# A later issue of packed query/key copies, and memory attention in three parts, in a hybrid transformer layer on one Trainium2 core

## The chip, the cores and the metric

The kernel runs on one core of one Trainium2 chip. The metric is the device time of one execution in microseconds (us), lower is better. Five engines work beside each other: PE (TensorE, matmuls; its weight loads are listed as PEld), DVE (VectorE), ACT (ScalarE), POOL (GpSimd) and SP (SyncE, which here only issues DMAs). Each takes its instructions in the order in which the program lists them for it.

## What is computed

One layer over 4096 tokens of width 1024: `x + W_out(concat(branches))`, where all branches read one normalised input.

```python
h = rms(x); g_u,g_v,g_gate, a_q,a_k,a_v,a_gate, m_q,m_gate = split(h @ w_in)
y_g = chunked_gmlp(g_u, rms(g_v)) * silu(g_gate)              # 4 heads x 64
y_a = dilated_attention(rms(a_q), rms(a_k), a_v) * silu(a_gate)   # 8 heads x 64, dilations 1, 4, 16
y_m = memory_attention(rms(m_q), mem) * silu(m_gate)          # 4 heads x 64, 256 memory tokens
x = x + concat([y_g, y_a, y_m]) @ w_out
```

The dilated attention is a softmax over a causal window for each of three dilations, mixed by the softmax denominators. The memory attention is a softmax over the 256 memory tokens.

## The kernel before, in words

The tokens are worked through in 32 tiles of 128. Every fp32 product is made of fp16 high and low parts, so that a projection (`proj`, L219) of one tile and 512 columns is 24 matmuls, accumulated in one PSUM buffer of the tag "pj", of which there are two.

Four stages follow each other. **Pass A** (L384) normalises and transposes each tile, writes it to DRAM, and projects the attention values (`pv`) and the queries and keys of heads 0 to 3 (`pq`). **Pass B** (`pass_b`, L678) loads the transposed tiles again and projects the queries and keys of heads 4 to 7 (`pqb`) and the attention gate (`pag`). **Pass C** (`pass_c`, L847) has three projections a tile: `pc1` (L855: the gMLP's v and the memory queries, wC1), `pc2` (L881, wC2) and `pc3` (L891, wC3). The last two belong to the tile that is LAG = 2 behind. The **output stage** (L934) adds the branches and projects with W_out. Beside passes B and C a side stream (`attn_all`, L660) computes the dilated attention: a maximum for each query (`attn_max`, L465: matmuls `pa`, DVE's L483) and the main part (`attn_main`, L533: matmuls `s`, DVE's mask L578, ACT's exponential L580 and cast `ph` L529, POOL's rest `pl` L530, matmuls `o`). `merge` (L59) advances the side stream by so many steps each time the pass yields, and gives its instructions a priority 400 places ahead.

The order on every engine is made by a scheduler ahead of the run: it simulates the program and gives an engine, of the instructions that are ready in that simulation, the one that comes first in program order (shifted by the priority). On the chip an engine then keeps that list, whether its next instruction is ready or not.

**Queries and keys** (`qk_out`, L292, in passes A and B). ACT copies the projection out of PSUM (L257) and squares it (L259); DVE sums (L261); POOL raises to the power -1/2 (L269); DVE multiplies (L276, L278); ACT casts the high half (`cast` below, L296), DVE makes the low half (L297). SP then issues a DMA that transposes `hl` into half of the staging tile `stg` (L299). ACT copies this half, its tokens regrouped by residue, into `stp` (L300). In every odd tile SP issues three stores of the pair of tiles to DRAM: L304 (keys), L305 (queries), both from `stg`, and L306 (packed, from `stp`). `stg` has two buffers, `stp` one. After every eighth tile of pass A `load_max` loads head 0's part of this back.

**Attention to the memory** (`mem_attn`, L776, in pass C, run after pc1). First part: ACT makes the high half `qd` (L779), DVE the low half in `q2t` (L780; a single buffer), SP issues the DMA transpose of `qd` (L784); matmuls `mpa` (L789) and DVE's L791 find each query's maximum, L792 writes it into `q2t`, and SP issues the DMA transpose of `q2t` (L793). Then a yield. Second part: the score matmuls `ms` (L802 and L804, the latter reads the transposed `q2t`), the exponential (L814), cast (L815), rest (L816), matmuls `mo` (L822 to L826), and the division (L829, L830). Then pc2 and pc3 of the tile two behind. The PSUM copy of pc1, `rw_c` (L257), has two buffers, and the memory queries are read out of it until L780.

Of the kernel before, what the change touches and what calls it, by code (L numbers as in the profile page):

```python
# [2 lines left out]

# [15 lines left out]
P = 128  # L19
T = 4096  # L20
D = 1024
NT = T // P
KT = D // P
# [17 lines left out]
R16 = 16  # L41
# [30 lines left out]
def tile_hybrid_layer(ctx, tc, x, mem, norm_gain, w_in, gv_gain, wsT, gb, aqg, akg,  # L72
# [146 lines left out]
    def proj(ps, xt, w, n, c=0):  # L219
        for k in range(KT):  # L220
            for a, b in ((0, 0), (0, 1), (1, 0)):
                TE.matmul(ps[:, :n], xt[:, a, k, :], w[:, b, k, c:c + n],  # L222
                          start=(k == 0 and a == 0 and b == 0), stop=(k == KT - 1 and a == 1))


    def load_rows(pool, src, nm):
# [62 lines left out]
    sk = ctx.enter_context(tc.tile_pool(name="sk", bufs=2))  # L289
    pm = ctx.enter_context(tc.tile_pool(name="pm", bufs=2))  # L290

    def qk_out(pool, ps, n, g, scs, stgs):  # L292
        stg, stp = stgs
        qn = qk_split(pool, ps, 8, scs, f"q{g}_{n}", agn, 4)
        hl = pool.tile([P, 8, 2, HD], F16, name=f"hl{g}_{n}", tag="hl", bufs=2)
        S.copy(hl[:, :, 0, :], qn)  # L296
        V.tensor_sub(hl[:, :, 1, :], qn, hl[:, :, 0, :])  # L297
        half = slice((n % 2) * P, (n % 2 + 1) * P)
        Q.dma_start_transpose(stg[:, :, half], hl.rearrange("p s a c -> p (s a c)"))  # L299
        S.copy(stp[:, :, half].rearrange("p s (r j) -> p s r j", r=R16),  # L300
               stg[:, :, half].rearrange("p s (j r) -> p s r j", r=R16))
        if n % 2 == 1:
            cc = slice((n - 1) * P, (n + 1) * P)
            Q.dma_start(kn_d[g][:, :, cc].rearrange("s p t -> p s t"), stg[:, 4:8, :])  # L304
            Q.dma_start(qn_d[g][:, :, cc].rearrange("s p t -> p s t"), stg[0:64, 0:4, :])  # L305
            Q.dma_start(qkp_d[g][:, :, cc].rearrange("s p t -> p s t"), stp)  # L306

    def stages(n):
        return (pm.tile([P, 8, 256], F16, name=f"stg{n}", tag="stg", bufs=2),
# [27 lines left out]
    with tc.tile_pool(name="pA", bufs=2) as pA:  # L337
# [44 lines left out]
        stg = None  # L382
        mTs = sk.tile([P, 2, 2, KT, P], F16, name="mTs", tag="q1", bufs=1)
        for n in range(NT):  # L384
# [46 lines left out]
                stg = stages(f"A{n}")  # L431
            qk_out(pm, ps, n, 0, scQ0, stg)
            if n % 8 == 7:
                load_max(0, (n - 7) * P, (n + 1) * P)
            tick()
            if n == 5:
# [237 lines left out]
    LAG = 2  # L674
# [3 lines left out]
    def pass_b():  # L678
        xTs = {}
        wQ1, scQ1 = got("wQ1")  # L680
        stg = None
        for n in range(NT + LAG):
            if n < NT:
                xT = sk.tile([P, 2, KT, P], F16, name=f"xTb{n}", tag="xT", bufs=4)
                Q.dma_start(xT.rearrange("p a k t -> p (a k t)"), xT_d[n])
                xTs[n] = xT
                ps = ps_tile("pj", [P, 512], F32, f"pqb{n}")
                proj(ps, xT, wQ1, 512)
                if n % 2 == 0:
                    stg = stages(f"B{n}")  # L690
                qk_out(pm, ps, n, 1, scQ1, stg)
                yield
            tick()
            if n == 2:
                wAG, scAG = got("wAG")
                for i in range(2):
                    V.tensor_scalar_mul(hsc[:, i:i + 1], scAG[i][:, 2:3], 0.5)
                    V.tensor_mul(fag[:, i:i + 1], hsc[:, i:i + 1], scV[i][:, 0:1])
                    V.tensor_scalar_mul(fag[:, i:i + 1], fag[:, i:i + 1], 2.0 ** -4)
            if n >= LAG:  # L700
                m = n - LAG
                ps = ps_tile("pj", [P, 512], F32, f"pag{m}")
                proj(ps, xTs.pop(m), wAG, 512)
                sg = pm.tile([P, 512], F32, name=f"sg{m}", tag="sg", bufs=2)
                for i in range(2):
                    S.activation(sg[:, i * 256:(i + 1) * 256], ps[:, i * 256:(i + 1) * 256],
                                 AF.Tanh, scale=hsc[:, i:i + 1])
                V.scalar_tensor_tensor(sg, sg, 1.0, ps, ALU.add, ALU.mult)
                Q.dma_start(ag_d[m], sg)
                yield  # L710
            if n == 6:
                start_job("wC1", "w1", (C_GV, C_MQ), ng, nga)
            if n == 16:
                start_job("wC3", "wc", (C_MG,), ng, nga)
            if n == NT - 1 + CS:
                start_job("wC2", "w2", (C_GU, C_GG), ng, nga, gap=1)
# [59 lines left out]
    def mem_attn(n, qn):  # L776
# [5 lines left out]
            qms[0] = pm.tile([P, 2, 2, 4, P], F16, name=f"qm{n}", tag="stg", bufs=2)  # L782
        Q1m, Q2m = qms[0][:, n % 2, 0], qms[0][:, n % 2, 1]
        Q.dma_start_transpose(Q1m, qd.rearrange("p s a c -> p (s a c)"))  # L784
        m4 = pm.tile([P, 4], F32, name=f"m4{n}", tag="m4")
        for hp in range(2):
            pa = ps_tile("pa", [P, 2, 256], F32, f"mpa{n}_{hp}")
            for i in range(2):
                TE.matmul(pa[:, i, :], Q1m[:, 2 * hp + i, :], K1m[:, 2 * hp + i, :],  # L789
                          start=True, stop=True)  # L790
            V.tensor_reduce(m4[:, 2 * hp:2 * hp + 2], pa, AX.X, ALU.max)  # L791
        V.tensor_scalar(q2t[:, :, 64], m4, -(2.0 ** -15), msg[:, 3:4], ALU.mult, ALU.add)  # L792
        Q.dma_start_transpose(Q2m, q2t.rearrange("p s c -> p (s c)"))  # L793
        yield
        o = ps_tile("po", [P, 4, 65], F32, f"mo{n}")
        for hp in range(2):
            st = ps_tile("ps", [P, 2, 2, P], F32, f"ms{n}_{hp}")
            for i in range(2):
                h = 2 * hp + i
                for b in range(2):  # L800
                    kk = slice(b * P, (b + 1) * P)
                    TE.matmul(st[:, i, b, :], K1m[:, h, kk], Q1m[:, h, :], start=True,  # L802
                              stop=False)
                    TE.matmul(st[:, i, b, :], K2m[:, h, kk], Q2m[0:65, h, :], start=False,  # L804
                              stop=True)
            if not pools:
                e = at.tile([P, 512], F32, name=f"me{n}_{hp}", tag="e", bufs=4)
                ph = at.tile([P, 512], F16, name=f"mph{n}_{hp}", tag="ph", bufs=4)
                pl = at.tile([P, 512], F16, name=f"mpl{n}_{hp}", tag="pl", bufs=4)
            else:  # L810
                e = pools[0].tile([P, 512], F32, name=f"me{n}_{hp}", tag="fx", bufs=3)
                phl = pools[0].tile([P, 2, 512], F16, name=f"mp{n}_{hp}", tag="fx", bufs=3)
                ph, pl = phl[:, 0, :], phl[:, 1, :]
            S.activation(e, st.rearrange("p a b q -> p (a b q)"), AF.Exp, scale=msg[:, 2:3])  # L814
            S.copy(ph, e)  # L815
            G.tensor_sub(pl, e, ph)  # L816
            for i in range(2):
                h = 2 * hp + i
                for b in range(2):
                    c = (2 * i + b) * P  # L820
                    v = Vm[:, b, h, :]
                    TE.matmul(o[:, h, 0:65], ph[:, c:c + P], v[:, 0:65], start=(b == 0),  # L822
                              stop=False)
                    TE.matmul(o[:, h, 0:64], ph[:, c:c + P], v[:, 66:130], start=False,
                              stop=False)
                    TE.matmul(o[:, h, 0:65], pl[:, c:c + P], v[:, 0:65], start=False,  # L826
                              stop=(b == 1))
        rd = pm.tile([P, 4], F32, name=f"rd{n}", tag="rd")
        V.reciprocal(rd, o[:, :, 64])  # L829
        V.tensor_tensor(ym[n], o[:, :, 0:64], bcast(rd, HD), ALU.mult)  # L830
        yield

    ym, vns = {}, {}
    o1 = []
# [12 lines left out]
    def pass_c():  # L847
        xTs = {}
        for n in range(NT + LAG):
# [15 lines left out]
            if n == 1:  # L865
                wC2, scC2 = got("wC2")
                V.tensor_scalar_mul(fz[:, 0:1], scC2[1][:, 2:3], 0.5)
                V.tensor_mul(fz[:, 1:2], fz[:, 0:1], scC2[0][:, 2:3])
                V.tensor_scalar_mul(fz[:, 2:3], scC3[0][:, 2:3], 0.5)
                V.tensor_mul(fz[:, 3:4], fz[:, 2:3], scM[1][:, 0:1])  # L870
                V.tensor_scalar_mul(fz[:, 3:4], fz[:, 3:4], 2.0 ** -4)
            if n < NT:
                yield from mem_attn(n, qn)
            if n >= LAG:
                m = n - LAG
                xT = xTs.pop(m)
# [1 line left out]
                    zp = pm.tile([P, 2, 256], F32, name=f"z{m}", tag="sg", bufs=2)  # L878
                z = zp[:, m % 2]
                ps = ps_tile("pj", [P, 512], F32, f"pc2_{m}")  # L880
                proj(ps, xT, wC2, 512)  # L881
                S.activation(z, ps[:, 256:512], AF.Tanh, scale=fz[:, 0:1])
                V.scalar_tensor_tensor(z, z, 1.0, ps[:, 256:512], ALU.add, ALU.mult)
                V.scalar_tensor_tensor(z, z, fz[:, 1:2], ps[:, 0:256], ALU.mult, ALU.mult)
                yield
                ps = ps_tile("pj", [P, 512], F32, f"pc3_{m}")
                pg = ps[:, 256:512].rearrange("p (h c) -> p h c", c=HD)
                vn = vns.pop(m)
                for h in range(4):
                    TE.matmul(pg[:, h, :], wst_g[:, h, :], vn[:, h, :], start=True, stop=True)  # L890
                proj(ps, xT, wC3, 256)  # L891
                for h in range(4):
                    V.scalar_tensor_tensor(z[:, h * HD:(h + 1) * HD], pg[:, h, :],
                                           gbt[:, h:h + 1], z[:, h * HD:(h + 1) * HD],
# [3 lines left out]
                S.activation(zm, ps[:, 0:256], AF.Tanh, scale=fz[:, 2:3])  # L898
                V.scalar_tensor_tensor(zm, zm, 1.0, ps[:, 0:256], ALU.add, ALU.mult)  # L899
                zms[m] = zm  # L900
                yield
            if n >= LAG + MLAG:
                mem_gate(n - LAG - MLAG)
# [87 lines left out]
```

## Time and profile before

| | us |
|---|---|
| runs before, median of 3 | 2227.14 |
| lowest and highest of them | 2226.68 and 2234.79 |
| the profiled execution, its own time | 2231.72 |
| span of the profiled execution, first to last instruction | 2230.0 |
| PE busy in it | 2031.2 (91%) |
| DVE busy | 1459.8 (65%) |
| ACT busy | 1200.2 (54%) |
| POOL busy | 684.2 (31%) |
| mean granted TensorE clock | 0.966 of full speed |

A busy figure is the union of an engine's instructions. An idle time is given to the instruction that ended it, with what released that instruction behind an arrow. The profile tells the granted clock of TensorE as a share of 2.4 GHz; 0.5 is its lower level of 1.2 GHz. Stages, read from the first and last projections of each: pass A from 52 to 458 us, pass B to 1016, pass C to about 1870, then the output stage.

### The profile page before, as it was taken

Reading aid. Unit: us, or ns where it says so; the run is one execution under the profiler, and the core shown is the slowest. Engines: PE = TensorE matmul, PEld = TensorE weight load, DVE = VectorE, ACT = ScalarE, POOL = GpSimd, SP = SyncE. Lnnn points to the kernel's source line nnn. Section 1 sums busy time; section 2 is a strip of 40 time slices with the busy share of each in tenths; the row PEclk is TensorE's granted clock in tenths of the full one; section 3 lists DMA queues with packets and bytes.
Section 4 is the critical chain, followed back from the end, with each engine's and each line's share of the span. In section 5 each row is a group of like instructions: output and inputs, shape, how many; then the busy total and the mean of one; then the engine's idle time right before and its main releaser. Section 6 shows DMA issues by size and latency. Waiting matters only on the chain. (4 is left out here: it accounts for less than half of the span.)

```text
span 2230.0 us, 45732 instructions
## 1 busy us (share of the span) xinstructions
PE 2031.2 (91%) x17025; PEld 1297.4 (58%) x17025; DVE 1459.8 (65%) x4331; ACT 1200.2 (54%) x2048; POOL 684.2 (31%) x632
## 2 busy tenths in 40 slices
PE   5989989889889898899999898998997999999999
PEld 4435444334346455465676675775764766666676
DVE  7555564365657676477786677875876667777662
ACT  6666565343457577476565565664655763222221
POOL 1212212121035355253454453553543551000000
PEclk8999999999899999999999999999998999999999
DMA  7767676484565865755646447536435337777662
GB/s 228 198 152 207 167 187 163 115 212 121 153 145 136 205 147 130 202 119 146 167 98 138 116 94 169 114 94 151 97 90 124 89 97 219 222 218 220 205 187 75
DMA packets 468959, 341.00 MB, mean 153 GB/s; under 512 B 294400, under 2 KB 404096, under 8 KB 466944
## 3 DMA queue, kind: packets, MB, share of 16 engines
q1 hardware_dynamic: 468736, 338.08, 58.8%
q8 instruction: 133, 2.18, 0.4%
q14 instruction: 90, 0.74, 0.1%
HBM read 198.52 MB, written 113.84 MB: 140 GB/s over the span
## 5 line engine op out<-in xcount | busy, mean ns | idle before, releaser
L530 POOL TENSOR_TENSOR pl<-e,ph 128x512 f16<-128x512 f32 (+1 forms) x384 | 413.1, 1088 | 359.2 <-ACT ph L529 265.2
L222 PE MATMUL pc<-wC,xTc 128*128 128x512 f16 (+1 forms) x2304 | 473.3, 349 | 6.3 <-DVE zm L899 5.2
L483 DVE CUSTOM_DVE_ANT_0 jk<-pa,mask 128x256 bf16<-128x256 f32 (+1 forms) x768 | 299.8, 390 | 86.1 <-PE pa L476 66.2
L222 PE MATMUL fps<-wO,fyT 128*128 128x256 f16 (+1 forms) x2304 | 341.0, 309 | 0.3 <-DVE fa L746 0.3
L222 PEld LDWEIGHTS <-xTc 128*128 128x128 f16 x2304 | 221.5, 100 | 161.6 <-issue 16.8
L580 ACT ACTIVATE e<-e,gas 128x512 f32<-128x512 f32 (+1 forms) x384 | 254.0, 674 | 112.5 <-DVE e L578 110.5
L578 DVE TENSOR_TENSOR e<-s,mask 128x512 f32<-128x512 f32 (+1 forms) x384 | 234.1, 626 | 77.8 <-PE s L575 68.3
L222 PEld LDWEIGHTS <-fyT 128*128 128x128 f16 x2304 | 224.5, 98 | 103.3 <-issue 1.7
L222 PEld LDWEIGHTS <-xTa 128*128 128x128 f16 x1608 | 159.4, 100 | 205.8 <-issue 42.3
L222 PEld LDWEIGHTS <-xTb 128*128 128x128 f16 x1536 | 150.8, 100 | 174.3 <-issue 29.1
L269 POOL TENSOR_TENSOR r_q<-r_q,mhalf 128x8 f32<-128x8 f32 x64 | 113.2, 1769 | 422.5 <-DVE r_q L267 406.9
L529 ACT CAST ph<-e 128x512 f16<-128x512 f32 (+1 forms) x384 | 211.9, 568 | 18.0 <-PE o L600 11.7
L222 PE MATMUL pqb<-wQ,xTb 128*128 128x512 f16 x768 | 191.6, 393 | 8.6 <-DMA xTb<-xTd 8.2
L222 PE MATMUL pag<-wAG,xTb 128*128 128x512 f16 x768 | 191.6, 389 | 8.0 <-ACT rw_q L257 4.3
L573 PE MATMUL s<-q,k 128*128 128x256 f16 (+1 forms) x768 | 178.8, 264 | 17.9 <-DVE e L578 7.0
L222 PE MATMUL pv<-wV,xTa 128*128 128x512 f16 (+1 forms) x840 | 180.8, 373 | 13.6 <-DVE vt L285 13.0
L222 PE MATMUL pq<-wQ,xTa 128*128 128x512 f16 x768 | 176.0, 385 | 18.3 <-ACT rw_q L257 15.3
L596 PE MATMUL o<-vr,ph 128*128 128x65 f16 x1368 | 173.0, 194 | 7.2 <-ACT ph L529 7.0
L476 PE MATMUL pa<-kp,qn 128*128 128x256 f16 (+1 forms) x768 | 137.8, 270 | 41.4 <-DVE mx L483 25.3
L575 PE MATMUL s<-q,k 65*128 65x256 f16 (+1 forms) x768 | 171.2, 264 | 1.9 <-DMA q<-cm 1.9
L598 PE MATMUL o<-vr,ph 128*128 128x64 f16 x1368 | 171.0, 194 | 0.0
L600 PE MATMUL o<-vr,pl 128*128 128x65 f16 x1368 | 161.1, 193 | 8.4 <-POOL pl L530 7.8
(282 smaller groups left out, 3356.5 us busy)
## 6 DMA issues: line engine op xcount, KB each, us to landing
vr<-vd SPq DMA_DIRECT2D x48, 520.0 KB
fo<-od SPq DMA_DIRECT2D x96, 260.0 KB
od<-ot SPq DMA_DIRECT2D x128, 130.0 KB
x_a<-in_x_dram SPq DMA_DIRECT2D x32, 512.0 KB
xTd<-xTa SPq DMA_DIRECT2D x32, 512.0 KB
xTb<-xTd SPq DMA_DIRECT2D x32, 512.0 KB
xTc<-xTd SPq DMA_DIRECT2D x32, 512.0 KB
fx<-in_x_dram SPq DMA_DIRECT2D x32, 512.0 KB
```

Of the source, the lines that this page charges most:

```text
L222: TE.matmul(ps[:, :n], xt[:, a, k, :], w[:, b, k, c:c + n], start=(k == 0 and a == 0 and b == 0), stop=(k == KT - 1 and a == 1))
L476: TE.matmul(pa[:, i, 256 - w:256], qn[:, q0:q0 + (P - 1) * d + 1:d], packed(kp, d, r, max(b - 1, 0), w), start=True, stop=True)
L483: V.tensor_tensor_reduce(jk[:, :w], pa[:, i, 256 - w:256], masks[d][:, 256 - w:256], 1.0, -3e38, ALU.add, ALU.max, mx[:, mc:mc + 1])
L529: S.copy(ph[:, :w], e[:, :w])
L530: G.tensor_sub(pl[:, :w], e[:, :w], ph[:, :w])
L573: TE.matmul(st[:, i, :n], k1[:, kk], packed(q1, d, r, b, n), start=True, stop=False)
L575: TE.matmul(st[:, i, :n], k2[:, kk], packed(q2, d, r, b, n), start=False, stop=True)
L578: V.tensor_tensor(e[:, :w], st.rearrange("p a q -> p (a q)")[:, :w], masks[d][:, :w], ALU.add)
L580: S.activation(e[:, :w], e[:, :w], AF.Exp, scale=asg[:, 2:3])
L596: TE.matmul(o[:, slot, 0:65], hi[:, c:c + 128], v[:, 0:65], start=(j == 0), stop=False)
L598: TE.matmul(o[:, slot, 0:64], hi[:, c:c + 128], v[:, 66:130], start=False, stop=False)
L600: TE.matmul(o[:, slot, 0:65], lo[:, c:c + 128], v[:, 0:65], start=False, stop=(j == len(terms) - 1))
```

## The change

`qk_out` no longer issues the packed copy L300 and the stores L304 to L306 itself: it puts them into a list, `late`, and the list is emptied (`flush`) in the next tile's `qk_out`, between that tile's DVE subtraction and its DMA transpose. There the ACT copies get an order edge behind that tile's cast (L296): ACT must issue them after it, without waiting for its end. The DMAs in the list get no edge. After every eighth tile of pass A and at the end of pass B the list is emptied in the same tile, without an edge.

`mem_attn` is cut in three: up to the DMA transpose of `qd`; from `mpa` to the DMA transpose of `q2t`; from `ms` to the end. They come before pc2, after pc2 and after pc3 of the tile two behind. `mpa` gets an order edge behind the last matmul of pc2, `ms` behind the last of pc3. The first two tiles have no such projections and get no edge. The number of yields a tile is as before.

```diff
@@ -219,8 +219,10 @@
     def proj(ps, xt, w, n, c=0):
         for k in range(KT):
             for a, b in ((0, 0), (0, 1), (1, 0)):
-                TE.matmul(ps[:, :n], xt[:, a, k, :], w[:, b, k, c:c + n],
-                          start=(k == 0 and a == 0 and b == 0), stop=(k == KT - 1 and a == 1))
+                last = TE.matmul(ps[:, :n], xt[:, a, k, :], w[:, b, k, c:c + n],
+                                 start=(k == 0 and a == 0 and b == 0),
+                                 stop=(k == KT - 1 and a == 1))
+        return last.ins
 
 
     def load_rows(pool, src, nm):
@@ -289,21 +291,33 @@
     sk = ctx.enter_context(tc.tile_pool(name="sk", bufs=2))
     pm = ctx.enter_context(tc.tile_pool(name="pm", bufs=2))
 
+    late = []
+
+    def flush():
+        while late:
+            late.pop(0)()
+
     def qk_out(pool, ps, n, g, scs, stgs):
         stg, stp = stgs
         qn = qk_split(pool, ps, 8, scs, f"q{g}_{n}", agn, 4)
         hl = pool.tile([P, 8, 2, HD], F16, name=f"hl{g}_{n}", tag="hl", bufs=2)
-        S.copy(hl[:, :, 0, :], qn)
+        cast = S.copy(hl[:, :, 0, :], qn)
         V.tensor_sub(hl[:, :, 1, :], qn, hl[:, :, 0, :])
+        with tc.issue_after(cast.ins):
+            flush()
         half = slice((n % 2) * P, (n % 2 + 1) * P)
         Q.dma_start_transpose(stg[:, :, half], hl.rearrange("p s a c -> p (s a c)"))
-        S.copy(stp[:, :, half].rearrange("p s (r j) -> p s r j", r=R16),
-               stg[:, :, half].rearrange("p s (j r) -> p s r j", r=R16))
-        if n % 2 == 1:
-            cc = slice((n - 1) * P, (n + 1) * P)
-            Q.dma_start(kn_d[g][:, :, cc].rearrange("s p t -> p s t"), stg[:, 4:8, :])
-            Q.dma_start(qn_d[g][:, :, cc].rearrange("s p t -> p s t"), stg[0:64, 0:4, :])
-            Q.dma_start(qkp_d[g][:, :, cc].rearrange("s p t -> p s t"), stp)
+
+        def pack(n=n, g=g, stg=stg, stp=stp, half=half):
+            S.copy(stp[:, :, half].rearrange("p s (r j) -> p s r j", r=R16),
+                   stg[:, :, half].rearrange("p s (j r) -> p s r j", r=R16))
+            if n % 2 == 1:
+                cc = slice((n - 1) * P, (n + 1) * P)
+                Q.dma_start(kn_d[g][:, :, cc].rearrange("s p t -> p s t"), stg[:, 4:8, :])
+                Q.dma_start(qn_d[g][:, :, cc].rearrange("s p t -> p s t"), stg[0:64, 0:4, :])
+                Q.dma_start(qkp_d[g][:, :, cc].rearrange("s p t -> p s t"), stp)
+
+        late.append(pack)
 
     def stages(n):
         return (pm.tile([P, 8, 256], F16, name=f"stg{n}", tag="stg", bufs=2),
@@ -431,6 +445,7 @@
                 stg = stages(f"A{n}")
             qk_out(pm, ps, n, 0, scQ0, stg)
             if n % 8 == 7:
+                flush()
                 load_max(0, (n - 7) * P, (n + 1) * P)
             tick()
             if n == 5:
@@ -690,6 +705,8 @@
                     stg = stages(f"B{n}")
                 qk_out(pm, ps, n, 1, scQ1, stg)
                 yield
+            if n == NT - 1:
+                flush()
             tick()
             if n == 2:
                 wAG, scAG = got("wAG")
@@ -782,16 +799,18 @@
             qms[0] = pm.tile([P, 2, 2, 4, P], F16, name=f"qm{n}", tag="stg", bufs=2)
         Q1m, Q2m = qms[0][:, n % 2, 0], qms[0][:, n % 2, 1]
         Q.dma_start_transpose(Q1m, qd.rearrange("p s a c -> p (s a c)"))
+        ins = yield
         m4 = pm.tile([P, 4], F32, name=f"m4{n}", tag="m4")
         for hp in range(2):
             pa = ps_tile("pa", [P, 2, 256], F32, f"mpa{n}_{hp}")
-            for i in range(2):
-                TE.matmul(pa[:, i, :], Q1m[:, 2 * hp + i, :], K1m[:, 2 * hp + i, :],
-                          start=True, stop=True)
+            with after(ins):
+                for i in range(2):
+                    TE.matmul(pa[:, i, :], Q1m[:, 2 * hp + i, :], K1m[:, 2 * hp + i, :],
+                              start=True, stop=True)
             V.tensor_reduce(m4[:, 2 * hp:2 * hp + 2], pa, AX.X, ALU.max)
         V.tensor_scalar(q2t[:, :, 64], m4, -(2.0 ** -15), msg[:, 3:4], ALU.mult, ALU.add)
         Q.dma_start_transpose(Q2m, q2t.rearrange("p s c -> p (s c)"))
-        yield
+        ins = yield
         o = ps_tile("po", [P, 4, 65], F32, f"mo{n}")
         for hp in range(2):
             st = ps_tile("ps", [P, 2, 2, P], F32, f"ms{n}_{hp}")
@@ -799,10 +818,11 @@
                 h = 2 * hp + i
                 for b in range(2):
                     kk = slice(b * P, (b + 1) * P)
-                    TE.matmul(st[:, i, b, :], K1m[:, h, kk], Q1m[:, h, :], start=True,
-                              stop=False)
-                    TE.matmul(st[:, i, b, :], K2m[:, h, kk], Q2m[0:65, h, :], start=False,
-                              stop=True)
+                    with after(ins):
+                        TE.matmul(st[:, i, b, :], K1m[:, h, kk], Q1m[:, h, :], start=True,
+                                  stop=False)
+                        TE.matmul(st[:, i, b, :], K2m[:, h, kk], Q2m[0:65, h, :], start=False,
+                                  stop=True)
             if not pools:
                 e = at.tile([P, 512], F32, name=f"me{n}_{hp}", tag="e", bufs=4)
                 ph = at.tile([P, 512], F16, name=f"mph{n}_{hp}", tag="ph", bufs=4)
@@ -828,7 +848,9 @@
         rd = pm.tile([P, 4], F32, name=f"rd{n}", tag="rd")
         V.reciprocal(rd, o[:, :, 64])
         V.tensor_tensor(ym[n], o[:, :, 0:64], bcast(rd, HD), ALU.mult)
-        yield
+
+    def after(ins):
+        return nullcontext() if ins is None else tc.issue_after(ins)
 
     ym, vns = {}, {}
     o1 = []
@@ -869,8 +891,10 @@
                 V.tensor_scalar_mul(fz[:, 2:3], scC3[0][:, 2:3], 0.5)
                 V.tensor_mul(fz[:, 3:4], fz[:, 2:3], scM[1][:, 0:1])
                 V.tensor_scalar_mul(fz[:, 3:4], fz[:, 3:4], 2.0 ** -4)
+            ma, ins = iter(()), None
             if n < NT:
-                yield from mem_attn(n, qn)
+                ma = mem_attn(n, qn)
+                next(ma)
             if n >= LAG:
                 m = n - LAG
                 xT = xTs.pop(m)
@@ -878,17 +902,21 @@
                     zp = pm.tile([P, 2, 256], F32, name=f"z{m}", tag="sg", bufs=2)
                 z = zp[:, m % 2]
                 ps = ps_tile("pj", [P, 512], F32, f"pc2_{m}")
-                proj(ps, xT, wC2, 512)
+                ins = proj(ps, xT, wC2, 512)
                 S.activation(z, ps[:, 256:512], AF.Tanh, scale=fz[:, 0:1])
                 V.scalar_tensor_tensor(z, z, 1.0, ps[:, 256:512], ALU.add, ALU.mult)
                 V.scalar_tensor_tensor(z, z, fz[:, 1:2], ps[:, 0:256], ALU.mult, ALU.mult)
                 yield
+            if n < NT:
+                ma.send(ins)
+                yield
+            if n >= LAG:
                 ps = ps_tile("pj", [P, 512], F32, f"pc3_{m}")
                 pg = ps[:, 256:512].rearrange("p (h c) -> p h c", c=HD)
                 vn = vns.pop(m)
                 for h in range(4):
                     TE.matmul(pg[:, h, :], wst_g[:, h, :], vn[:, h, :], start=True, stop=True)
-                proj(ps, xT, wC3, 256)
+                ins = proj(ps, xT, wC3, 256)
                 for h in range(4):
                     V.scalar_tensor_tensor(z[:, h * HD:(h + 1) * HD], pg[:, h, :],
                                            gbt[:, h:h + 1], z[:, h * HD:(h + 1) * HD],
@@ -898,6 +926,13 @@
                 S.activation(zm, ps[:, 0:256], AF.Tanh, scale=fz[:, 2:3])
                 V.scalar_tensor_tensor(zm, zm, 1.0, ps[:, 0:256], ALU.add, ALU.mult)
                 zms[m] = zm
+                yield
+            if n < NT:
+                for _ in (0,):
+                    try:
+                        ma.send(ins)
+                    except StopIteration:
+                        pass
                 yield
             if n >= LAG + MLAG:
                 mem_gate(n - LAG - MLAG)
```

## Rows read from the trace of the kernel before

**Rows 1.** Stages: stretch, length, engines' busy us (count), PEclk, DMA share, GB/s.

```profile
52.00:458.00 406.00, 369.98 (x2012) 180.50 (x2013) 206.72 (x480) 236.69 (x331) 78.65 (x87) 0.97 0.67 170
458.00:1016.00 558.00, 496.32 (x3797) 284.77 (x3796) 365.94 (x1244) 331.07 (x576) 197.13 (x164) 0.95 0.63 158
1016.00:1870.00 854.00, 783.93 (x8267) 562.71 (x8265) 621.69 (x1951) 506.84 (x985) 397.36 (x349) 0.97 0.51 121
```

**Rows 2.** Waits in pass A, 52 to 458: total us, times, longest.

```profile
ACT stpA L300 <- DMA stgA<-hl: 95.1, 27, 9.8
...
ACT hl L296 <- DVE rw_q L278: 30.2, 14, 4.3
PE pq L222 <- ACT rw_q L257: 15.3, 10, 2.4
PE pv L222 <- DVE vt L285: 13.0, 3, 8.9
```

**Rows 3.** Timeline in pass A: start, us, engine, instruction, [idle before].

```profile
255.71 2.04 ACT L300 COPY stpA<-stgA 128x1024 f16<-128x1024 f16 x1 [7.95 <-DMA stgA<-hl]
257.65 0.58 ACT L257 COPY rw_q<-pq 128x512 f32<-128x512 f32 x1
...
258.28 5.34 PE L222 MATMUL pq<-wQ,xTa 128*128 128x512 f16 x24 [1.00 <-ACT rw_q L257]
...
280.36 2.25 SPq L299 DMA_TRANSPOSE stgA<-hl  x1
...
286.83 2.02 ACT L300 COPY stpA<-stgA 128x1024 f16<-128x1024 f16 x1 [9.83 <-DMA stgA<-hl]
...
295.59 4.75 PE L222 MATMUL pv<-wV,xTa 128*128 128x512 f16 x14 [8.94 <-DVE vt L285]
```

**Rows 4.** Busy time and clock just after that gap, columns as in rows 1.

```profile
292.00:299.00 7.00, 3.41 (x9) 1.23 (x9) 4.99 (x10) 4.66 (x9) 0.62 (x2) 0.52 0.63 199
```

**Rows 5.** Waits in pass B, 458 to 1016.

```profile
ACT stpB L300 <- DMA stgB<-hl: 98.8, 28, 8.9
...
ACT hl L296 <- DVE rw_q L278: 43.2, 18, 8.5
...
PE pqb L222 <- DMA xTb<-xTd: 8.2, 5, 3.2
PE o L596 <- ACT ph L529: 7.0, 10, 1.2
...
PE pag L222 <- ACT rw_q L257: 4.3, 2, 2.7
```

**Rows 6.** Timeline of SP in pass B, 902 to 945.

```profile
931.88 0.39 SPq L304 DMA_DIRECT2D knd<-stgB  x1
...
933.60 0.37 SPq L306 DMA_DIRECT2D qkpd<-stpB  x1
...
934.75 2.46 SPq L685 DMA_DIRECT2D xTb<-xTd  x2
```

**Rows 7.** Waits in pass C, 1016 to 1870.

```profile
DVE q2t L780 <- DMA qm<-q2t: 51.3, 19, 8.7
...
ACT rw_c L257 <- DVE q2t L780: 28.3, 8, 11.4
...
PE ms L804 <- DMA qm<-q2t: 24.0, 5, 15.0
```

**Rows 8.** Lines L882 and L789 from 1016: duration ns, first, last start.

```profile
L882 ACT ACTIVATE z<-pc,fz x9: 455/474/482, 1053.0 to 1254.8; 128x256 f32<-128x256 f32 x9
...
L789 PE MATMUL mpa<-K1m,qm x44: 270/272/282, 1046.8 to 1313.2; 128*128 128x256 f16 x44
```

**Rows 9.** Timeline of SP in pass C, 1670 to 1696.

```profile
1690.54 1.27 SPq L793 DMA_TRANSPOSE qm<-q2t  x1
```

**Rows 10.** Timeline of DVE in pass C, 1670 to 1696.

```profile
1674.96 0.42 DVE L792 TENSOR_SCALAR q2t<-m,gms 128x4 f16<-128x4 f32 x1
...
1694.67 0.42 DVE L780 TENSOR_TENSOR q2t<-rw_c,qd 128x256 f16<-128x256 f32 x1 [4.41 <-DMA qm<-q2t]
```

More of the change, by code (lines that the diff above doesn't have):

```diff
@@ L1 @@
 import math
-from contextlib import ExitStack
+from contextlib import ExitStack, nullcontext
 import concourse.bass as bass
```

## The prediction

> **What bounds the kernel now.** I read first the busy time cut by stage, then the waits of each stage that the change touches, then the timeline around the longest of them. By stage the reader is to see that PE is the engine that is nearly always at work, and how much it idles: 36.0 us of pass A's 406, 61.7 of pass B's 558 and 70.1 of pass C's 854 (length less busy time), while ACT is busy for 58 and 59% of the first two stages [rows 1]. So only a wait that reaches PE is worth anything. The waits of pass A say what reaches it: ACT stands for 95.1 us in front of the packed copy L300, 27 times, until the transposing DMA has landed, and PE stands for 15.3 us in ten waits for ACT's PSUM copy `rw_q` and for 13.0 in three waits for `vt`, 8.9 of them in one [rows 2]. The timeline joins the two: the DMA is issued at 280.36, ACT goes on only at 286.83 after idling 9.83 us, and PE gets its buffer at 295.59, 8.94 us late; at 255.71 the same stall and the 2.04 us of the copy itself put `rw_q` behind them, and PE loses 1.00 us [rows 3]. ACT keeps its order, so work that is ready stands behind a copy whose data is late. After the long gap the granted clock was 0.52 in a stretch of 7 us, the lower of the two levels, 1.2 GHz [rows 4].
>
> **The change, part by part.** No instruction is added or taken away: 64 copies, 64 transposing DMAs and 96 stores stay, each at its own time. What changes is their place.
>
> *Copies in pass A.* Tile n's copy now stands behind tile n+1's cast. Between the transposing DMA's issue and that cast lies about a tile, 406/32 = 12.7 us; the one landing read here took 286.83 - 280.36 = 6.5. So the ACT wait goes, except in the tiles 7, 15, 23 and 31, whose list is emptied at once. The copy's 2.04 us stay, on an engine that idles 42% of the stage, beside PE's blocks of 24 matmuls, 5.34 us each [rows 3]. Of PE's waits 15.3 + 8.9 = 24.2 us are at stake [rows 2]. I take off 4/32 for those tiles, leaving 21. The slow clock costs more: 14 matmuls took 4.75 us where 24 take 5.34 at the full clock (14 would take 3.1), so 1.6 us at this gap alone [rows 3]. At most it could give back (1 - 0.97) x 406 = 12.2 us [rows 1]. I take 3, near the lower end, as I have read only one such gap out. Pass A: 24 us, between 0, if all its waits return elsewhere, and 36.0 + 12.2 = 48. Next late is the cast itself, for which ACT waits 30.2 us [rows 2].
>
> By the Trainium skill, "DMA: Bandwidth & Descriptors", sections "Anatomy of one DMA" and "Latency and other measured facts", a DMA has about 2.0 us of fixed time (fitted on another issuing path) and a transposing one moves 261 GB/s; for the 262 KB here my estimate is 3.0 us. By it ACT would have gone on at about 283.4, the long gap would not be there and pass A's term would lose 9 us; the trace has 6.5, and decides.
>
> *Copies in pass B.* ACT waits 98.8 us, but the side stream fills PE meanwhile. Surely tied to it are PE's 4.3 us for `rw_q` [rows 5] and one late load: SP stands at L304 until 931.88 and at L306 until 933.60, and only then, at 934.75, issues the two loads of `xTb` [rows 6], for which PE waits up to 3.2 us [rows 5]. Of the 7.0 us for the cast `ph`, which follows the copy on ACT, I count half. That makes 4.3 + 3.2 + 3.5 = 11 us; the bounds are 0 and 4.3 + 8.2 + 7.0 = 19.5.
>
> *Stores, and SP's queue.* L304 to L306 move behind a whole tile of other DMA issues and stand ahead of the next L299. Their data is then ready but for L306, whose copy is at most two ACT instructions away. SP issues L304 and L306 in about 0.4 us each [rows 6], and nobody needs the data in DRAM before the lists are emptied. `stg` has two buffers of two tiles each, so that holding one for a tile longer costs nothing; `stp` is written again only a tile after its store. If that cover went, the copy would wait for the store's landing, as it waits for the transposing DMA today. POOL's queue has nothing moved past it.
>
> *Memory attention.* Two edges. They ask for what is so already: 44 `mpa` matmuls are 11 tiles of four, and tile 10's last starts at 1313.2; ACT's ninth `z`, which follows pc2 of tile 8, its partner, starts at 1254.8 [rows 8]. `mpa` is 58 us behind the matmul that it is now tied to, so the edge itself costs nothing and gives nothing. What moves is the place in the simulated order: `mpa` and L793 fall behind pc2 and one more piece of the side stream, `ms` behind pc3. This may win back PE's 24.0 us in front of `ms` [rows 7]. But 15.0 of these came about otherwise: L792 had written `q2t` by 1675.4, SP came to L793 only at 1690.54, and the data landed for L780 at 1694.67 [rows 9, 10]; SP's queue held it, and SP is not tied by the edges. On the other side DVE waits 51.3 us, 19 times, with L780 for this same DMA, and ACT 28.3 us for DVE [rows 7]; a later L793 makes both longer. Bounds: a gain of 24.0, a loss of 28.3 if ACT's wait doubles and all of it reaches PE. I take 0, in the middle, as the rows show a cause on either side.
>
> *Sum.* 24 + 11 + 0 = 35 us. The profiled execution took 2231.72 us, 1.7 outside its span and 4.6 above the median of the runs. Against the median: 2227.14 - 35 = 2192 us.
>
> **The rivals.** *Pass C gains too* (0.17): the order moves L793 and `ms` apart and the 24.0 us go. Speaking for it: two pieces of PE's work more lie between them. Against: the late SP. Time: 2192 - 24 = 2168.
>
> *The waits come back* (0.15): the edge holds a copy that is ready behind a cast that is not; ACT waits 30.2 us for casts in pass A and 43.2 in pass B [rows 2, 5]. Then cast, copy and `rw_q` stand in a row, and PE still waits where the cast's delay and the copy's 2.04 us outlast its 5.34 us block. Only the one long gap goes: 2227.14 - 8.9 = 2218, no change that can be told.
>
> *The chain over `q2t` becomes the bound, slower* (0.10). `q2t` is a single buffer: L793 of a tile must land before the next L780, L780 frees `rw_c` for the tile after that, and so pc1. If each of the 19 waits of today grows by half of a pc2 block, 2.7 us (the other half filled by the side stream), that is 51 us, and 2192 + 51 = 2243. It decides for slower once pass C loses more than 35 + 11 = 46 us. Against it: `mpa` was long after pc2 anyhow. By the Trainium skill, "Perfetto Trace Analysis", section "Tensor Engine Instruction", ACT's and DVE's queues are strictly first in, first out; a wait of L780 then stops the side stream's masks behind it, and PE with them, as ACT's 28.3 us behind DVE agree with [rows 7].
>
> *The change does not do what it says* (0.03): only ACT's and PE's instructions carry edges, and a scheduler that reorders the rest can keep the waits as they were: 2227.
>
> **How the numbers follow.** The forecast has the remaining 0.55. A measurement here can tell about 0.5%, 11 us, from no change. Faster: the forecast, *pass C gains* and a little of the third case, 0.74; the same: 0.15; slower: 0.11. The range reaches from 2162, a little under the case in which pass C gains, to 2236, above the cases of no change, and leaves out most of the slower one and gains in A and B near their upper bounds.
>
> **What would show it.** Right: ACT's wait for `stg` falls from some 200 us to under 30, in five copies alone; PE's idle time in pass A falls to about 15 us, with hardly a wait for `rw_q`; SP's waits at L304 are gone; pass C's length stays within 15 us of 854. Wrong: PE's waits of pass A return behind the cast or behind POOL; pass C grows, with L780's wait above 51 us; or PE's wait for `ms` vanishes. As the whole order is simulated anew, waits that the change does not touch can fall elsewhere too, by some us.

## The result, and the profile after

The change takes 2151.44 us (median of 4 runs, 2146.65 to 2156.89) where the kernel before takes 2230.43 (median of 4): a ratio of 0.9646, interval 0.9614 to 0.9678. That is 79 us less, more than twice the 35 forecast, and below the range. The profiled execution of the change took 2156.89 us with a span of 2155.2. All twelve experiments below ran later, against the kernel before at 2241 to 2243 us, 0.5% more than here; they are therefore compared by their ratios.

Busy time by stage of the change, each stage cut at the same event as in [rows 1] (pass C's end 10.5 us after its last projection); columns as there:

```profile
52.00:426.00 374.00, 363.24 (x2013) 179.04 (x2013) 206.95 (x481) 236.16 (x328) 80.73 (x87) 0.98 0.74 184
426.00:959.00 533.00, 487.93 (x3816) 285.56 (x3814) 367.16 (x1245) 333.16 (x584) 197.83 (x165) 0.96 0.68 168
959.00:1797.00 838.00, 786.51 (x8262) 565.40 (x8261) 631.81 (x1957) 508.50 (x982) 397.10 (x348) 0.97 0.51 124
```

Pass A is 32 us shorter, pass B 25, pass C 16. In pass A PE idles 10.8 us where it idled 36.0, and it is busy for 6.7 us less with the same work, at a granted clock of 0.98. In pass B the idle time falls from 61.7 to 45.1 and the busy time by 8.4. In pass C the idle time falls from 70.1 to 51.5.

Waits of the change in pass A (52 to 426), which answer to [rows 2]:

```profile
ACT hl L304 <- DVE rw_q L280: 29.0, 18, 5.3
...
ACT stpA L312 <- DMA stgA<-hl: 8.5, 4, 3.5
...
PE pq L222 <- DVE wQ L174: 3.8, 1, 3.8
PE pv L222 <- DVE vt L287: 3.8, 3, 2.2
```

PE's ten waits for `rw_q` are gone, and the long one for `vt`. ACT's wait at the copy fell from 95.1 us to 8.5, in four copies: those of the tiles whose list is emptied at once (over both passes it is 18.8 us in seven copies, where the prediction had five). The timeline of the change in pass A shows the new rhythm, PE without a gap and the copy directly behind the cast, with nothing to wait for:

```profile
240.72 5.34 PE L222 MATMUL pq<-wQ,xTa 128*128 128x512 f16 x24
...
241.95 0.62 ACT L304 CAST hl<-rw_q 128x512 f16<-128x512 f32 x1 [0.43 <-DVE rw_q L280]
242.48 2.05 ACT L312 COPY stpA<-stgA 128x1024 f16<-128x1024 f16 x1
...
246.10 0.58 ACT L259 COPY rw_q<-pq 128x512 f32<-128x512 f32 x1 [1.58 <-PE pq L222]
...
251.97 5.34 PE L222 MATMUL pq<-wQ,xTa 128*128 128x512 f16 x24
...
258.05 5.34 PE L222 MATMUL pv<-wV,xTa 128*128 128x512 f16 x24
...
259.24 2.04 ACT L312 COPY stpA<-stgA 128x1024 f16<-128x1024 f16 x1 [3.46 <-DMA stgA<-hl]
...
263.23 5.34 PE L222 MATMUL pq<-wQ,xTa 128*128 128x512 f16 x24
```

A tile takes 251.97 - 240.72 = 11.25 us here; now ACT waits for PE. The copy at 259.24 is one of the four that are emptied at once: ACT waits 3.46 us, and PE's next block still follows without a gap.

PE's waits of the change in pass B (426 to 959), which answer to [rows 5]:

```profile
PE o L611 <- ACT ph L544: 2.4, 3, 1.1
PE pag L222 <- ACT rw_q L259: 2.1, 2, 2.0
```

And in pass C (959 to 1800), to [rows 7]:

```profile
PE ms L824 <- DMA qm<-q2t: 7.3, 4, 2.3
```

The load of `xTb` is no longer among pass B's waits at all. In pass C PE's 24.0 us for `ms` have become 7.3.

### The profile page after: what moved, and what is told of

Read it like the earlier page. It is cut to its first block, busy times and chain, and to the rows that moved or that the text cites. A ratio compares the mean times of both kernels' runs of the same rounds, so it can differ in the third digit from the quotient of the medians.

```text
span 2155.2 us, 45734 instructions
## 1 busy us (share of the span) xinstructions
PE 2015.6 (94%) x17025; PEld 1297.5 (60%) x17025; DVE 1465.5 (68%) x4331; ACT 1202.0 (56%) x2048; POOL 686.3 (32%) x632
## 5 line engine op out<-in xcount | busy, mean ns | idle before, releaser
L222 PE MATMUL pc<-wC,xTc 128*128 128x512 f16 (+1 forms) x2304 | 479.5, 350 | 1.1 <-DMA xTc<-xTd 0.8
```

The costliest lines, as they stand in the source:

```text
L222: last = TE.matmul(ps[:, :n], xt[:, a, k, :], w[:, b, k, c:c + n], start=(k == 0 and a == 0 and b == 0), stop=(k == KT - 1 and a == 1))
```

## The experiments

Stages below are cut at PE's first `pqb`, first `pc` and last `pc` matmul, and pass A is counted from 52 us; the columns of the table are lengths in us from one profile of each kernel, ACT's total wait at the packed copy for the transposing DMA (both passes, from the waits of the whole span), and PE's wait for `ms`.

| kernel | ratio to before | A | B | C | ACT at the copy | PE for ms |
|---|---|---|---|---|---|---|
| before | 1 | 406 | 558 | 843 | 203 | 24 |
| the change | 0.965 | 374 | 533 | 827 | 19 | 7 |
| late_only | 0.962 | 374 | 527 | 833 | 19 | 3 |
| mem_only | 0.996 | 413 | 561 | 839 | 205 | 4 |
| late_no_edge | 0.998 | 416 | 564 | 842 | 210 | 5 |
| mem_no_edge | 0.963 | 375 | 525 | 831 | 18 | 5 |
| copy_no_wait2 | 0.978 | 372 | 520 | 869 | 0 | 14 |
| late_A | 0.975 | 377 | 565 | 815 | 90 | 4 |
| late_B | 0.982 | 412 | 538 | 822 | 110 | 2 |
| stores_in_place | 0.964 | 378 | 535 | 825 | 19 | 4 |
| before_hp | 1.000 | 411 | 558 | 847 | 199 | 25 |
| before_hp2 | 0.992 | 414 | 554 | 821 | 188 | 14 |
| q2t_two | 0.964 | 372 | 523 | 823 | 16 | 4 |
| late_all | 0.969 | 366 | 550 | 829 | 13 | 4 |

**late_only: the copies alone.** `mem_attn` and `pass_c` are those of before; the list and its edge stay.

> Only the copies and stores a tile later; memory attention as before. If the gain of passes A and B (57 us between the two profiles) is the copies' and that of pass C (about 16 us) the memory attention's: pass C keeps its length of 843 us, PE still waits about 24 us for ms, and the time is 2230 - 57 = 2173 us. If pass C's gain came with any new order, whatever the part: about 2155. If the parts need each other: over 2190.

2157.97 us, ratio 0.9623 (0.9608 to 0.9637): no less than the whole change gains. Pass C is shorter here too, and PE's wait for `ms` is 3.0 us, with the old memory attention. So the first expectation, that this wait belongs to the split, falls.

**mem_only: the memory attention alone.** `qk_out` is that of before; the three parts and their edges stay.

> Only the memory attention in three parts with its edges; copies as before. If the split is what takes PE's wait for ms away: passes A and B as before, pass C 16 us shorter, 2214 us, and PE's wait for ms under 10 us. If the edges are idle because mpa and ms already came later, and the wait for ms is decided by SP's queue at the change of heads: 2230 within 8 us, with the wait for ms anywhere between 5 and 30.

2234.84 us, ratio 0.9963 (0.9943 to 0.9984), a gain of 0.4%. PE's wait for `ms` fell to 4.2 us, and pass C is only 5 us shorter than in the profile of before: 20 us less of this wait brought hardly any time. The waits of mem_only, over the whole span:

```profile
ACT stpA L302 <- DMA stgA<-hl: 106.5, 29, 10.1
ACT stpB L302 <- DMA stgB<-hl: 98.3, 28, 8.3
...
PE ms L809 <- DMA qm<-q2t: 4.2, 4, 2.3
```

**late_no_edge: the later copies without their order edge.**

```diff
-        with tc.issue_after(cast.ins):
-            flush()
+        flush()
```

> The whole change but without the order edge of the copies behind the cast: the scheduler may put a copy wherever its simulation has it ready, which is up to three ACT instructions ahead of the cast. If the later place in program order is enough: within 6 us of the change's 2151. If the edge carries it: ACT's wait for stg comes back in part, 60 us or more, and half of the gain of passes A and B goes, 2180.

2236.85 us, ratio 0.9977 (0.9955 to 0.9998): almost nothing is left. Its waits, over the whole span:

```profile
ACT stpA L311 <- DMA stgA<-hl: 109.1, 28, 11.9
ACT stpB L311 <- DMA stgB<-hl: 101.4, 29, 8.5
...
PE pqb L222 <- DMA xTb<-xTd: 9.4, 6, 3.9
```

Its timeline in pass A shows why. The copy, a tile later in the program, was pulled up again, ahead of `rw_q`, and ACT stands in front of it for the DMA (that the simulation had its data ready there follows from the scheduler's rule; the simulated times are in no trace):

```profile
254.09 0.62 ACT L304 CAST hl<-rw_q 128x512 f16<-128x512 f32 x1
...
255.47 3.68 SPq L308 DMA_TRANSPOSE stgA<-hl  x1
...
262.83 2.03 ACT L311 COPY stpA<-stgA 128x1024 f16<-128x1024 f16 x1 [8.12 <-DMA stgA<-hl]
264.76 0.58 ACT L259 COPY rw_q<-pq 128x512 f32<-128x512 f32 x1
...
265.39 5.34 PE L222 MATMUL pq<-wQ,xTa 128*128 128x512 f16 x24 [1.39 <-ACT rw_q L259]
```

The edge, not the later line, is what takes the wait away.

**mem_no_edge: the three parts without their edges.** `after(ins)` returns an empty context.

> The whole change but without the order edges on mpa and ms. If they are idle, since mpa runs tens of us behind pc2 anyway: 2151 within 6 us, passes A and B the same. If they hold ms back until its DMA has landed: PE's wait for ms returns, 24 us, 2168.

2158.17 us, ratio 0.9626 (0.9611 to 0.9641); PE's wait for `ms` 5.0 us. These edges are idle, as [rows 8] had it.

**copy_no_wait2: the copy in its old place, with no DMA to wait for.** On the kernel before; the copy reads the tile `hl` from before the transpose, so that this kernel leaves the transposition of the packed data out and computes something else:

```diff
-        S.copy(stp[:, :, half].rearrange("p s (r j) -> p s r j", r=R16),
-               stg[:, :, half].rearrange("p s (j r) -> p s r j", r=R16))
+        S.activation(stp[:, :, half].rearrange("p s (r j) -> p s r j", r=R16),
+                     hl.rearrange("p s a c -> p s (a c)").rearrange("p s (j r) -> p s r j", r=R16),
+                     AF.Copy, scale=2.0 ** -8)
```

> The kernel before with the packed copy in its old place, but reading hl, which is in SBUF, instead of the transposed stg; so the packed queries and keys are other numbers, scaled down by 2^-8, and the dilated attention computes something else. Same copy, no wait for a DMA. If ACT's wait for the transposing DMA is the whole cause: ACT's wait at the copy near zero, and the ratio to the kernel before that of the later copies alone, 0.962, in passes A, B and C alike. If the copy's place behind the cast, the more regular order, does part of it: 0.975 or more.

Pass A did as the first expectation says: 372 us. Pass B took 520 us, but not all of that is the wait. The rows of its passes B and C, and of pass C before (columns as in [rows 1]):

```profile
424.00:944.00 520.00, 475.84 (x3630) 275.03 (x3629) 349.29 (x1198) 318.29 (x552) 186.75 (x155) 0.96 0.68 168
944.00:1812.70 868.70, 798.98 (x8343) 572.58 (x8342) 623.49 (x1947) 513.20 (x1004) 405.96 (x358) 0.96 0.50 117
1016.00:1859.50 843.50, 774.33 (x8204) 557.00 (x8202) 611.46 (x1921) 504.32 (x982) 397.36 (x349) 0.97 0.50 121
```

PE did 3630 matmuls in pass B here and 3797 before; the work that is missing moved, most of it to pass C (8343 against 8204). What can be compared is PE's idle time in pass B: 44.2 us, as in the change (45.1), against 61.7 before. So the wait for the DMA is the cause of pass A's gain and of pass B's idle time, and neither the copy's own 2 us nor another place for it is needed. (ACT still waits 34.3 us at these copies, for DVE's low half of `hl`.) The ratio is nevertheless 0.978 (0.9747 to 0.9814), where the second expectation lies, as pass C took 869 us, longer than in any other kernel: 25 us of that are the work moved there, and its idle time, 69.7 us, is that of before (69.2), while the change has 51.5. Its numbers differ in this kernel, but PE's list is made ahead of the run, so that it is the other order that moved the work; why pass C idles no less was not tried.

**late_A and late_B: one pass at a time.** On late_only, for g = 0 and g = 1:

```diff
-        late.append(pack)
+        if g == 0:
+            late.append(pack)
+        else:
+            pack()
```

> Copies and stores a tile later in pass A alone, memory attention as before. If each pass gains by its own copies: pass A 32 us shorter, pass B as before within 6, and pass C too; ratio 0.985. If passes B and C gained because any new order suits them: pass B and C shorter as well, ratio under 0.975.

> Copies and stores a tile later in pass B alone. If each pass gains by its own copies: pass A as before, pass B 25 to 32 us shorter; pass C tells whether its 11 to 16 us follow from pass B (then they come here, ratio 0.982) or from nothing in particular (then they need not, 0.988).

late_A 2184.24 us, 0.9748 (0.9724 to 0.9772); late_B 2199.03 us, 0.9817 (0.9784 to 0.9851). Each pass gains by its own copies: pass A is 377 us with them and 412 without, pass B 538 with and 565 without. Pass C came out at 815 and 822 us, among the shortest of all (before_hp2 has 821), and it did so with copies late in pass A alone, or in pass B alone: late_A's ratio is better than its 0.985 because pass C gains 28 us there, nearly as much as pass A. The instructions of PE's projections in pass B of late_A (ns, then first and last start, forms):

```profile
L222 PE MATMUL pqb<-wQ,xTb x768: 376/379/634, 429.3 to 964.6; 128*128 128x512 f16 x192
```

The same of its pass C, which begins at 994.0:

```profile
L222 PE MATMUL pc<-wC,xTc x2304: 270/379/634, 994.0 to 1809.3; 128*128 128x512 f16 x128, 128*128 128x256 f16 x64
```

And of pass C of late_B, whose pass B begins at 464.2:

```profile
L222 PE MATMUL pc<-wC,xTc x2304: 270/379/634, 1002.6 to 1824.6; 128*128 128x512 f16 x128, 128*128 128x256 f16 x64
```

**stores_in_place: the plain stores not late.** On late_only, the stores of `kn_d` and `qn_d` are issued where they were, L306 stays in the list.

> Copies and packed stores a tile later, but the stores of plain keys and queries at their old place, so that SP again stands in its queue until the transposing DMA has landed. If ACT's wait is all: ratio 0.962, SP's waits back at about 60 us. If SP's waits held back the loads of pass B: pass B gives back 5 to 15 us, PE waits for xTb again, ratio 0.967 or more.

2160.16 us, 0.9636 (0.9603 to 0.967). But this run is no contrast: both expectations take it that SP's wait for the transposing DMA had gone in the change, and it had not. Only the ACT copies carry the edge; the plain stores, which the program of the change has a tile later, were pulled up again. SP in pass A of the change, around an odd tile:

```profile
233.45 1.23 SPq L309 DMA_TRANSPOSE stgA<-hl  x1
236.20 0.37 SPq L316 DMA_DIRECT2D knd<-stgA  x1
...
243.32 1.32 SPq L309 DMA_TRANSPOSE stgA<-hl  x1
244.73 0.53 SPq L318 DMA_DIRECT2D qkpd<-stpA  x1
```

The store of keys is issued 2.75 us after their own tile's transposing DMA, and before the next tile's; only the packed store L318 comes a tile later. SP's own waits at the store of keys, over the whole span, in the kernel before, then in the change, then here:

```profile
SPq L304 <- DMA stgA<-hl: 42.4, 16, 4.0
...
SPq L304 <- DMA stgB<-hl: 15.6, 11, 3.4
```

```profile
SPq L316 <- DMA stgA<-hl: 41.4, 16, 3.9
...
SPq L316 <- DMA stgB<-hl: 18.3, 11, 2.9
```

```profile
SPq L312 <- DMA stgA<-hl: 44.3, 16, 3.7
...
SPq L312 <- DMA stgB<-hl: 19.8, 11, 3.2
```

That is 58, 60 and 64 us, and late_no_edge, which gains almost nothing, has 61. So this wait did not change with the time, and the gain does not come from it. PE does not wait for `xTb` in the change nor here; why that wait went stays open.

**before_hp and before_hp2: another order, nothing else.** `HP = 400` becomes 408 and 392.

> A control: the kernel before with the side stream's priority 408 places ahead in place of 400. Copies, stores and memory attention as before; only the simulated order is another. If pass C's length is chance of that order: passes A and B within 8 us of before, pass C anywhere between 815 and 850 us, PE's wait for ms anywhere between 2 and 25. If 843 us is what this memory attention takes: pass C within 5 us of it, ratio 0.998 to 1.002.

> The same control with 392 places. The same two expectations; the difference between the two controls is a measure of the chance in one new order.

2240.66 us, 0.9997 (0.9979 to 1.0015), and 2224.25 us, 0.992 (0.9893 to 0.9947). With 408 pass C took 847 us, with 392 821. The first and last starts of pass C's projections in before_hp:

```profile
L222 PE MATMUL pc<-wC,xTc x2304: 270/379/634, 1020.6 to 1867.2; 128*128 128x512 f16 x128, 128*128 128x256 f16 x64
```

The same in before_hp2:

```profile
L222 PE MATMUL pc<-wC,xTc x2304: 270/379/634, 1020.2 to 1841.6; 128*128 128x512 f16 x128, 128*128 128x256 f16 x64
```

PE's wait for `ms` in before_hp:

```profile
PE ms L804 <- DMA qm<-q2t: 25.1, 6, 15.8
```

And in before_hp2:

```profile
PE ms L804 <- DMA qm<-q2t: 14.2, 5, 5.5
```

A shift of 8 places in a priority can move this kernel by 0.8%, and pass C by more than the 16 us that it gained in the change.

**q2t_two and late_all: two attempts to go further.** On the change: two buffers for `q2t` (`q2ts[n % 2]`); and `load_max` of pass A put into the list, in place of the early `flush()`.

> The change, with two buffers for q2t in place of one. If the chain over q2t holds pass C (the rival of the prediction): DVE's 43 us of waiting there go to near zero, and pass C is 10 to 30 us shorter, 2125 to 2140 us beside the change's 2151. If PE is filled by the side stream anyway: DVE's wait goes and the time stays within the spread of one new order, ratio 0.958 to 0.970.

> The change, with the list no longer emptied at once after every eighth tile of pass A: the load of head 0's part goes into the list too. ACT's last 8.5 us of waiting in pass A go. If they still cost PE: pass A 2 to 5 us shorter. If they are hidden: pass A within 2 us, and the time within the spread of one new order.

q2t_two: 2159.13 us, 0.9639 (0.9614 to 0.9664). DVE's wait there fell only from 42.6 to 29.4 us, and the time is the change's. late_all: 2170.59 us, 0.9691 (0.9663 to 0.9718). Pass A did become 8 us shorter, 366, more than its first expectation had; PE idles 5.2 us there in place of 10.8. But pass B took 550, the longest of those with later copies in it; PE did 3931 matmuls there, 115 more than in the change, so that part of its length is work that moved from pass C. Neither beats the change. DVE's wait in q2t_two, over the whole span:

```profile
DVE q2t L798 <- DMA qm<-q2t: 29.4, 12, 5.3
```

## Why the prediction was wrong

*The direction and the mechanism* held: ACT's in-order wait for the transposing DMA reached PE, and its going is the gain. copy_no_wait2 shows it for passes A and B with the copy left in its place in the program, late_no_edge shows that the time comes back with the wait, and late_A and late_B show it for each pass by itself. For pass C it is not shown.

*The term for pass A*, 24 us, was too small: 32 in the two profiles. Of the idle time 25.2 us went where I had 21; I had taken off 3 for the tiles whose list is emptied at once, and the one in the timeline above cost PE nothing. (Whether all four did stays open: late_all, which empties none at once, has a pass A 8 us shorter, but it moves the loads behind them too.) PE's busy time fell by 6.7 us where I had 3: I had read the slow clock at one gap alone, which makes 1.6 of it. The kernel before has three more such blocks in pass A, each behind a wait for `vt` or `rw_q`:

```profile
138.75 6.83 PE L222 MATMUL pv<-wV,xTa 128*128 128x512 f16 x24 [3.36 <-DVE vt L285]
...
424.62 7.03 PE L222 MATMUL pq<-wQ,xTa 128*128 128x512 f16 x24 [1.85 <-ACT rw_q L257]
...
451.17 7.03 PE L222 MATMUL pq<-wQ,xTa 128*128 128x512 f16 x24 [2.43 <-ACT rw_q L257]
```

They are 1.5, 1.7 and 1.7 us longer than 5.34, which with the 1.6 makes 6.5 (each kernel has a slow stretch or two more, behind loads and weights); no block of the change's pass A behind such a wait is slow. The upper bound, 48, stands.

*The term for pass B*, 11 us, failed most: 25. The three waits that I had named fell from 19.5 us [rows 5] to 4.5, by 15, so that the bound which I had put at the top was nearly what happened; I had counted half of one and only the longest of another. And no clock was counted there: with the idle time 16.6 us shorter, PE's busy time fell by 8.4, at a granted clock of 0.96 where it was 0.95.

*The paragraph on the stores* failed as well: their data was to be ready when SP came to them, and SP's waits at L304 were to be gone. SP stands there for 60 us in the change and stood for 58, since nothing holds the plain stores late. So the late load of `xTb` [rows 6] may have had another cause than the one I gave; PE's 8.2 us for it went all the same.

*The term for the memory attention*, 0, was right by itself, as far as can be told: mem_only gains 0.4%, less than a new order alone can bring, and mem_no_edge shows that the edges are idle. But pass C was 16 us shorter for a reason that I had mentioned without giving it a price: the whole order is simulated anew. Kernels whose pass C is that of before took 815 to 847 us there (before, late_only, late_A, late_B, stores_in_place, before_hp, before_hp2; copy_no_wait2 with its other numbers apart), and the kernel before stood near the slow end. That before_hp2 has 821 with no copy late shows that an order alone can do it. It does not show that it was chance here: all eight kernels with copies held late, in one pass or in both, lie between 815 and 833 us, and of the five others with ACT's wait as before four lie between 839 and 847. What in the order makes pass C shorter stays open. The wait for `ms` is the same story: 25 us or 14 with the priority a few places apart, 4 and 5 in mem_only and late_no_edge, 2 to 7 in the kernels with later copies.

*The range* failed by these steps together: 32 + 25 + 16 = 73 of the 74.8 us between the two spans. I had let it reach only to the case in which pass C gains, and left out the upper bounds of passes A and B, although the text had them at 48 and 19.5, and what a new order alone can bring, 18 us in before_hp2. The chances do not follow from the rivals either: the 0.11 for slower is more than its one rival's 0.10, and the 0.15 for the same leaves out the 0.03 at 2227.

*The rivals.* That pass C gains too had the size nearly right, 24 us forecast against 16, by luck: in mem_only PE's wait for `ms` fell by 20 us and pass C by 5. The waits did not come back behind the cast: ACT's wait there in pass A is 29.0 us, about as before, and PE does not feel it. The chain over `q2t` did not become the bound: its wait fell to 42.6 us, and a second buffer gains nothing. The rival that the scheduler could undo the change is just what late_no_edge shows, and what happened to the plain stores; the edge is what rules it out for the copies, and I had given it too little attention.

*The figure of the Trainium skill* ("DMA: Bandwidth & Descriptors", sections "Anatomy of one DMA" and "Latency and other measured facts"), from which 3.0 us were worked out for a transposing DMA, would have left pass A's longest wait out. In late_no_edge 7.4 us lie between the issue at 255.47 and the copy at 262.83, as the 6.5 that the prediction had read. But the tile before, in the same trace, comes near the estimate, with 2.8 us from the issue to the copy that waits for it:

```profile
247.69 1.23 SPq L308 DMA_TRANSPOSE stgA<-hl  x1
...
250.45 2.05 ACT L311 COPY stpA<-stgA 128x1024 f16<-128x1024 f16 x1 [0.54 <-DMA stgA<-hl]
```

So the one landing that the prediction had read was a slow one; the runs show both, and the long waits come from the slow ones, as SP's own 3.68 us at 255.47, against 1.23 at 247.69, suggest.

## What to carry to other kernels

Where a scheduler orders the work by a simulation, look for the instructions that wait longest on an in-order engine for a DMA: the likely reason, which no trace shows, is that the simulation took that DMA to be quicker than it was. Moving such an instruction later in the program was not enough here, since it was pulled up again; an order edge behind a neighbour that is late enough held it (0.965 with it, 0.998 without). And look in the trace whether what was meant to move did: the plain stores had not. And before a small gain in an untouched stage is believed, run a control that changes nothing but the order: here that alone was worth up to 0.8%.

## What was not expected of the hardware

How much of the gain is clock. Between the two profiles PE did the same 17025 matmuls in 2031.2 and in 2015.6 us of busy time, 15.6 us less, and the mean granted clock rose from 0.966 to 0.974 of 2.4 GHz. So about a fifth of the 74.8 us between the spans came from PE standing at its lower level for a shorter time, once its waits were fewer, and not from the waits themselves. The other profiles agree: PE is busy for 2031 to 2047 us in the five kernels with ACT's wait as before, and for 2010 to 2021 in the six with the copies late in both passes. The waits that went with it were short: the slow blocks of pass A at 424.62 and 451.17 follow waits of 1.85 and 2.43 us, and the granted clock from 425.0 to 428.4 us was 0.51 (line below). A wait of that size does not always do it: in the change PE's 19 matmuls at 190.53 follow one of 2.25 us and take 4.26 us, as at the full clock.

```profile
425.00:428.40 3.40, 3.40 (x9) 1.17 (x8) 1.50 (x6) 1.07 (x4) 1.70 (x2) 0.51 0.91 257
```
